# The memory's values as a group of two weight blocks with seven products

## The chip, the cores and the metric

The kernel runs on one core of a Trainium2 chip. The metric is the time of one execution on the device in microseconds, here the median of several executions. TensorE (PE in the profile) multiplies matrices, VectorE (DVE), ScalarE (ACT) and GpSimd (POOL) work elementwise, and SyncE (SP) issues most of the DMAs. Each engine takes its instructions in a fixed order from a queue of its own, and waits on semaphores for the others.

## The reference

One layer of a hybrid decoder over 256 tokens of width 2048. The part that matters here is the cross-attention into 256 memory tokens, whose keys and values come from one projection:

```python
mem_kv = rmsnorm(mem, mem_norm[l]) @ w_mem_kv[l]
m_k, m_v = jnp.split(mem_kv, 2, axis=-1)
m_k = rmsnorm(m_k.reshape(B, M, MEM_HEADS, MEM_DH), mem_k_norm[l])
m_v = m_v.reshape(B, M, MEM_HEADS, MEM_DH)
```

`w_mem_kv` is 2048 x 2048: its first 1024 columns give the keys, the last 1024 the values. After that comes the big projection of `x` (its first part is the queries for the memory, `mq`), the other mixers, the merge and the feed-forward part. All of it is float32 in and out.

## The kernel before, in words

**Numbers.** A float32 product is made of three matmuls on rounded parts: each operand is split into a high part (rounded, by an ACT copy) and a low part (the rest, by a DVE subtract), and high x high, low x high and high x low are summed in PSUM. `split` (L151, L152) does that for weights and activations.

**Plain blocks.** `gemm` multiplies 256 tokens with a block of 512 weight columns. The 2048 rows are 16 chunks of 128. A load brings four chunks (1 MB) into a slot `raw`; two chunks at a time are split into a pair of tiles `wh`, `wl` (a part, 128x1024); each part feeds 12 matmuls (two chunks, two halves of the tokens, three products) of 128x512. There are four pairs of `wh`, `wl` in this stretch, so the split of a part waits until TensorE is through with the part four places back. The `raw` slots are a list, `free_raw`: a load takes the slot that came free first. At the start these are three slots of the pool `ring1` and three borrowed places: `sh` and `sl` of the pool `fpool` (the later home of the activations' forms) and `d` of the pool `sec`.

**Groups of two blocks.** `sgemm` multiplies the same tokens with two blocks of 512 columns at once. In the first eight chunks it can replace the eight products of a 2 x 2 arrangement (two halves of the tokens or of the chunks, two halves of the chunks or blocks) by seven, over `p` chunks of each four; the remaining chunks go through `rest` as in `gemm`. For the seven products it needs sums of activations (`make_forms`: four sums and differences, each split into high and low, in a background that is woven into the code that runs beside it), sums of weights (a DVE add of 128x1024 in place, L283, or an accumulating DMA from POOL, L331 and L351), and some moves in PSUM: `put` copies or subtracts a product from a `tmp` bank into an `acc` bank or a spare piece (L314, L316). Four `acc` banks and two `tmp` banks are in use at once, and up to four `raw` slots are held until their last use.

**The order.** A scheduler that orders the instructions when the program is built works from the code's order and from its own estimates; what it made of both kernels is shown under the change.

**The stretch of the change.** First the memory's keys, two plain blocks (`o`, `o1`), while the memory's activations `mems` (tiles `oh`, `ol`) are loaded as `xraw` and split, and its row norms are made. Then the memory's values `mv`, two plain blocks (`project`), while beside them the keys are normalised and transposed, and `x` is loaded and split (`xTh`, `xTl`). Then `mq`, two plain blocks, while the forms of `x` (`sx`) are made, and from there on groups of two blocks throughout.

Of the kernel before, what the change touches and what calls it, by code (L numbers as in the profile page):

```python
# [10 lines left out]
F32R = mybir.dt.float32r  # L11
# [5 lines left out]
P = 128  # L17
# [3 lines left out]
NB = 512  # L21
# [56 lines left out]
def trunk(ctx: ExitStack, tc: tile.TileContext, a, out):  # L78
# [118 lines left out]
    def gemm(xs, w, c0, row0=0, first=(), load=nc.sync.dma_start, fine=False):  # L197

        o = [acc() for _ in range(2)]
        nk = len(xs)
        sizes = list(first)
        sizes += [min(KG, nk - k) for k in range(sum(sizes), nk, KG)]
        k0 = 0
        for n in sizes:
            xp = [x() if callable(x) else x for x in xs[k0 : k0 + n]]
            raw, done = loads()  # L210
            r0 = row0 + k0
            load(raw[:, :n], w[c0 // NB, :, r0 : r0 + n])
            for g in range(0, n, 2):
                m = min(2, n - g)
                wh, wl = (x[:].rearrange("p (k n) -> p k n", k=2) for x in parts())
                split(wh[:, :m], wl[:, :m], raw[:, g : g + m])
                if g + m == n:
                    done()
                for t in range(2):
                    s = slice(t * P, (t + 1) * P)  # L220
                    for j in range(m):
                        xh, xl = xp[g + j]
                        k = k0 + g + j
                        pe.matmul(o[t][:], xh[:, s], wh[:, j], start=k == 0, stop=False)  # L224
                        pe.matmul(o[t][:], xh[:, s], wl[:, j], start=False, stop=False)  # L225
                        pe.matmul(o[t][:], xl[:, s], wh[:, j], start=False, stop=k == nk - 1)  # L226
                    if fine and t == 0:
                        step()
                step()
            k0 += n  # L230
        return o

    def sgemm(xs, forms, w, blks, p, row0=0, late=False, moved=True, base=None, end=False):
# [56 lines left out]
            return [[x[:, t * P : (t + 1) * P] for x in xs[h * SP + i]] for i in range(SP)]  # L290

        def formed(f):
            return [[x[:, f, i] for x in forms] for i in range(SP)]

        def made():
            while id(forms) in making:
# [113 lines left out]
    def form_tiles():  # L410
        return [fpool.tile([P, 4, SP, P], F32R, name=f"s{x}", tag=f"s{x}") for x in "hl"]

    def make_forms(parts, place):

        def add(dst, a, b, op=ALU.add):
            dve.tensor_tensor(dst, a, b, op=op)

        def make():  # L420
            a = {}
            for k in range(2):
                for i in range(2):
                    at = piece()
                    a[i, k] = at[:].rearrange("p (k t) -> p k t", k=SP)
                    n = 0
                    for h, l in parts:
                        m = h.shape[1]
                        lo, hi = max(k * SP, n), min((k + 1) * SP, n + m)
                        if lo < hi:  # L430
                            add(
                                a[i, k][:, lo - k * SP : hi - k * SP],
                                *(x[:, lo - n : hi - n, i * P : (i + 1) * P].bitcast(F32) for x in (h, l)),
                            )
                        n += m
                    yield
            a11, a12, a21, a22 = a[0, 0], a[0, 1], a[1, 0], a[1, 1]
            for f, dst, x, y, op in (
                (1, a21, a22, a21, ALU.subtract),
                (3, a22, a12, a22, ALU.subtract),  # L440
                (2, a12, a21, a12, ALU.subtract),
                (0, a11, a11, a12, ALU.add),
            ):
                add(dst, x, y, op)
                yield
                split(place[0][:, f], place[1][:, f], dst)
                yield
            making.remove(id(place))

        making.add(id(place))  # L450
        background.append(make())
        return place

# [40 lines left out]
    def evac(dst, o, rstd):  # L494

        for t in range(2):
            act.activation(dst[:, t], o[t][:], AF.Copy, scale=rstd[:, t : t + 1])

    def project(dst, xs, w, c0, rstd):
        for n in range(0, MIX, NB):  # L500
            evac(dst[:, :, n : n + NB], gemm(xs, w, c0 + n), rstd)

    def normed_T(dst, src, heads, dim, gain, scratch, wait=0):


# [62 lines left out]
        return t.rearrange("p a b -> p (a b)").rearrange("p (c t) -> p c t", c=8)  # L568


    free_raw.extend([(fpool, 1, "sh"), (fpool, 1, "sl"), (sec, 1, "d")])
    mk, mkT = section("mk", "a"), chunks(section("mkT", "b")[:])
    mv, mqT = pair("mv_mqT")
    mqT = chunks(mqT)
# [10 lines left out]
    def outT():  # L585
        return [opool.tile([P, 8, T], F32R, tag="o", name=f"o{x}", bufs=4) for x in "hl"]

    mems = load_T([outT(), outT()], a["memT"], g_mem, mempool)
    cst = const.tile([P, C_R], F32, name="cst")
    cr = const.tile([P, R_W], F32R, name="cr")  # L590
    r_mem, nr_mem, r_x, nr_x = (const.tile([P, 2], F32, name=n) for n in ("r_mem", "nr_mem", "r_x", "nr_x"))
# [20 lines left out]
    dve.tensor_scalar(g_sqs[:], gain["sb_q_norm"], SD**-0.5, None, op0=ALU.mult)  # L612

    background += [token_rstd("mem", a["mem"], r_mem, nr_mem), load_consts()]
    o1 = gemm(mems, w_kv, NB)
    flush()
    evac(mk[:, :, :NB], o, r_mem)
# [7 lines left out]
    background.append(normed_T(mkT, mk, MH, MD, g_mk, lambda: mempool.tile([P, NB], F32, name="hn_sq", tag="hn")))  # L625
    background.append(load_x())
    background.append(token_rstd("x", a["x"], r_x, nr_x))
    project(mv, mems, w_kv, MIX, r_mem)
    flush()
    xs = [x() for x in xs]  # L630
    give_up(fpool)
# [98 lines left out]
    def wide(dst, c0, p=SP):  # L730
        for j, result in sgemm(xs, sx, w_in, (c0 // NB, c0 // NB + 1), p):
            for t in range(2):
                v = dst[:, t, j * NB : (j + 1) * NB]
                act.activation(v, result(t), AF.Copy, scale=r_x[:, t : t + 1])

    sx = make_forms([xtiles], form_tiles())
    mq = section("mq", "d")
    evac(mq[:, :, :NB], gemm(xs, w_in, O_MQ), r_x)
# [488 lines left out]
```

## Time and profile before

| | us |
|---|---|
| median of 3 runs | 1612.01 (1611.77 to 1614.13) |
| the profiled execution, its own time | 1609.67 |
| span of the profiled execution (first to last instruction) | 1607.9 |
| TensorE busy in the span | 1600.4 |
| VectorE busy | 1354.9 |
| ScalarE busy | 1043.8 |

The profiled execution's own time is 1.8 us over its span (launch and end), and 2.3 us under the median. A matmul's record is longer than the distance to the next one, since matmuls overlap; how fast TensorE goes is read from the starts of the rows, not from their durations. The same holds for the elementwise engines on a smaller scale: the next one starts a little before the last one's record ends.

### The profile page before, as it was taken

The page shows a single profiled execution, that of the slowest core. Times are in us where ns is not written, and L with a number is a line of the kernel's source. Part 1 is how long each engine was busy: PE and PEld are TensorE (multiplying, and loading weights), DVE is VectorE, ACT ScalarE, POOL GpSimd, SP SyncE. Part 2 cuts the span into 40 slices and gives each one's busy share as a digit, 9 for nine tenths or more (in the row PEclk, how much of TensorE's full clock was granted, in tenths as well). Part 3 has the DMA queues.
Part 4 walks back from the last instruction along what each step waited for, and adds up shares of the span by engine and source line. Part 5 has one row for each costly group of instructions (what it writes and reads, how often), then busy time and mean ns, then how long its engine had stood idle before and what let it go on. Part 6 is the DMA issues. An engine that isn't in the chain of part 4 may idle for free.

```text
span 1607.9 us, 19413 instructions
## 1 busy us (share of the span) xinstructions
PE 1600.4 (100%) x7204; PEld 1315.0 (82%) x7204; DVE 1354.9 (84%) x1544; ACT 1043.8 (65%) x1273; POOL 73.0 (5%) x95
## 2 busy tenths in 40 slices
PE   9999999999999999999999999999999999999998
PEld 7888888888888888888888888888888888888887
DVE  6777788897776788897799998988878988888996
ACT  7765677776764666665656766666666666666663
POOL 0000000000000000000000000000000000110000
PEclk9999999999999999999999999999999999999999
DMA  9765768767556878887757868777898786897684
GB/s 377 299 263 168 233 216 262 216 171 255 197 182 218 263 256 264 265 287 287 238 182 261 272 227 256 260 249 236 258 281 260 219 276 231 250 280 242 201 320 128
DMA packets 66383, 394.18 MB, mean 245 GB/s; under 512 B 7344, under 2 KB 14128, under 8 KB 21488
## 3 DMA queue, kind: packets, MB, share of 16 engines
q1 hardware_dynamic: 51344, 323.31, 52.5%
q0 software_dynamic: 11792, 66.59, 21.7%
q10 hardware_dynamic: 3152, 3.04, 0.6%
q8 instruction: 56, 0.92, 0.2%
q14 instruction: 39, 0.32, 0.1%
HBM read 324.24 MB, written 12.58 MB: 209 GB/s over the span
## 4 chain that ended last, share of the span: by engine, by line
PE 96%; DMA 2%; ACT 1%; DVE 1%; issue 0%; SPq 0%; DVEq 0%; ACTq 0%; POOLq 0%
PE acc L268 19%; PE acc L271 19%; PE acc L270 19%; PE tmp L271 7%; PE tmp L270 7%; PE tmp L268 7%; PE acc L226 5%; PE acc L225 5%; PE acc L224 5%; PE tmp L455 2%; DMA raw<-in_w_down 1%; DMA raw<-raw 0%; PE tmp L693 0%; PE tmp L721 0%; ACT wh L151 0%; DMA raw<-in_w_mem_kv 0%
## 5 line engine op out<-in xcount | busy, mean ns | idle before, releaser
L152 DVE TENSOR_TENSOR wl<-raw,wh 128x1024 fp32r<-128x1024 f32 (+1 forms) x765 | 920.1, 1221 | 209.9 <-ACT wh L151 196.6
L151 ACT CAST wh<-raw 128x1024 fp32r<-128x1024 f32 (+1 forms) x766 | 796.6, 1050 | 442.2 <-PE acc L271 225.5
L268 PE MATMUL acc<-wh,xTh 128*128 128x512 f32 x480 | 190.5, 397 | 0.0
L270 PE MATMUL acc<-wl,xTh 128*128 128x512 f32 x480 | 187.2, 390 | 0.0
L271 PE MATMUL acc<-wh,xTl 128*128 128x512 f32 x480 | 186.9, 390 | 0.0
L268 PE MATMUL acc<-wh,hh 128*128 128x512 f32 x452 | 178.8, 395 | 0.0
L270 PE MATMUL acc<-wl,hh 128*128 128x512 f32 x452 | 176.0, 389 | 0.0
L271 PE MATMUL acc<-wh,hl 128*128 128x512 f32 x452 | 175.0, 390 | 0.0
L283 DVE TENSOR_TENSOR raw<-raw 128x1024 f32<-128x1024 f32 x133 | 161.4, 1221 | 1.1 <-DMA raw<-in_w_down 0.5
L224 PE MATMUL acc<-wh,oh 128*128 128x512 f32 x320 | 126.6, 397 | 0.9 <-ACT wh L151 0.9
L225 PE MATMUL acc<-wl,oh 128*128 128x512 f32 x320 | 125.1, 391 | 0.5 <-DVE wl L152 0.5
L226 PE MATMUL acc<-wh,ol 128*128 128x512 f32 x320 | 124.8, 390 | 0.0
L268 PE MATMUL tmp<-wh,sh 128*128 128x512 f32 x294 | 115.7, 394 | 0.0
L271 PE MATMUL tmp<-wh,sl 128*128 128x512 f32 x294 | 114.7, 390 | 0.0
L270 PE MATMUL tmp<-wl,sh 128*128 128x512 f32 x294 | 114.6, 390 | 0.0
L268 PEld LDWEIGHTS acc<-wh,xTh 128*128 128x128 f32 x480 | 90.2, 188 | 20.7 <-ACT acc L314 3.1
L271 PEld LDWEIGHTS acc<-wh,xTl 128*128 128x128 f32 x480 | 90.1, 188 | 19.0
L270 PEld LDWEIGHTS acc<-wl,xTh 128*128 128x128 f32 x480 | 90.2, 188 | 17.8
L268 PEld LDWEIGHTS acc<-wh,hh 128*128 128x128 f32 x452 | 84.9, 188 | 18.6 <-ACT acc L314 1.0
L271 PEld LDWEIGHTS acc<-wh,hl 128*128 128x128 f32 x452 | 84.8, 188 | 18.0
L270 PEld LDWEIGHTS acc<-wl,hh 128*128 128x128 f32 x452 | 84.9, 188 | 16.8
L268 PE MATMUL acc<-wh,fh 128*128 128x512 f32 x220 | 86.5, 394 | 0.2 <-ACT acc L314 0.2
(311 smaller groups left out, 2322.1 us busy)
## 6 DMA issues: line engine op xcount, KB each, us to landing
raw<-in_w_gate_up SPq DMA_DIRECT2D x88, 1024.0 KB, 6.3
raw<-in_w_in SPq DMA_DIRECT2D x56, 1024.0 KB, 5.8
raw<-raw POOLq DMA_DIRECT2D x52, 1024.0 KB, 8.0
raw<-in_w_gate SPq DMA_DIRECT2D x48, 1024.0 KB, 7.4
raw<-in_w_down SPq DMA_DIRECT2D x44, 1024.0 KB, 7.2
raw<-in_w_o SPq DMA_DIRECT2D x16, 1024.0 KB, 6.2
raw<-in_w_mem_kv SPq DMA_DIRECT2D x14, 1024.0 KB, 10.5
raw<-in_w_br_mem SPq DMA_DIRECT2D x8, 1024.0 KB, 5.6
```

Source lines behind the costliest of these rows:

```text
L151: act.copy(hi, src)
L152: dve.tensor_tensor(lo, src, hi.bitcast(F32), op=ALU.subtract)
L224: pe.matmul(o[t][:], xh[:, s], wh[:, j], start=k == 0, stop=False)
L225: pe.matmul(o[t][:], xh[:, s], wl[:, j], start=False, stop=False)
L226: pe.matmul(o[t][:], xl[:, s], wh[:, j], start=False, stop=k == nk - 1)
L268: pe.matmul(dst[:], xh, wh, start=id(dst) not in begun, stop=False, skip_group_check=True)
L270: pe.matmul(dst[:], xh, wl, start=False, stop=False, skip_group_check=True)
L271: pe.matmul(dst[:], xl, wh, start=False, stop=last, skip_group_check=True)
L283: dve.tensor_tensor(x, x, y, op=ALU.add)
L455: pe.transpose(dst, src, ident)
```

## The change

The two blocks of the values become one `sgemm` group with `p` = 2: of the chunks 0 to 3 and 4 to 7, two of each four go by seven products, and the others by `rest`. `make_forms` gets the number of chunks as an argument, and the memory's forms (`smem`) are put into the background beside the second block of the keys. Their place is `sh` of `fpool`, which is no longer a `raw` slot. The sums are made in pieces of the pool `gog`; leftover pieces are dropped before the forms of `x`.

```diff
@@ sgemm, make_forms
         def formed(f):
-            return [[x[:, f, i] for x in forms] for i in range(SP)]
+            return [[x[:, f, i] for x in forms] for i in range(p)]
...
-    def make_forms(parts, place):
+    def make_forms(parts, place, p=SP):
...
-                    a[i, k] = at[:].rearrange("p (k t) -> p k t", k=SP)
+                    a[i, k] = at[:].rearrange("p (k t) -> p k t", k=SP)[:, :p]
...
-                        lo, hi = max(k * SP, n), min((k + 1) * SP, n + m)
+                        lo, hi = max(k * SP, n), min(k * SP + p, n + m)
@@ slots and tiles
-    free_raw.extend([(fpool, 1, "sh"), (fpool, 1, "sl"), (sec, 1, "d")])
+    free_raw.extend([(fpool, 1, "sl"), (sec, 1, "d")])
...
-    mems = load_T([outT(), outT()], a["memT"], g_mem, mempool)
+    mtiles = [outT(), outT()]
+    mems = load_T(mtiles, a["memT"], g_mem, mempool)
@@ before the keys' second block
+    smem = fpool.tile([P, 2, 4, 2, P], F32R, name="smem", tag="sh")
+    smem = make_forms(mtiles[:1], [smem[:, 0], smem[:, 1]], 2)
     o1 = gemm(mems, w_kv, NB)
@@ the values
-    project(mv, mems, w_kv, MIX, r_mem)
+    mems = [x() for x in mems]
+    for j, result in sgemm(mems, smem, w_kv, (MIX // NB, MIX // NB + 1), 2):
+        for t in range(2):
+            act.activation(mv[:, t, j * NB : (j + 1) * NB], result(t), AF.Copy, scale=r_mem[:, t : t + 1])
@@ before the forms of x
+    halves.clear()
     sx = make_forms([xtiles], form_tiles())
```

In the lists below, taken from the two built programs, `wh_n` and `wl_n` are the high and low part of a piece of weights, `raw_n` a load's slot, `oh`, `ol` the memory's activations and `xraw` their loads, `two` a piece that holds a sum, `smem` the forms' place.

ScalarE in the first block of the keys, from the activations of the chunks 10 and 11 on, before:

```order
L154 ACTIVATE oh_113<-xraw_235,vecs_85 128x256 x2
L151 CAST wh_243<-raw_241 128x1024
L151 CAST wh_259<-raw_241 128x1024
L154 ACTIVATE oh_113<-xraw_275,vecs_85 128x256 x2
L154 ACTIVATE oh_113<-xraw_281,vecs_85 128x256 x2
L151 CAST wh_289<-raw_287 128x1024
```

and now:

```order
L154 ACTIVATE oh_113<-xraw_235,vecs_85 128x256 x2
L151 CAST smem_325<-two_435 128x256
L151 CAST smem_325<-two_472 128x256
L151 CAST wh_243<-raw_241 128x1024
L151 CAST wh_259<-raw_241 128x1024
L154 ACTIVATE oh_113<-xraw_275,vecs_85 128x256 x2
L154 ACTIVATE oh_113<-xraw_281,vecs_85 128x256 x2
L151 CAST smem_325<-two_472 128x256
L151 CAST smem_325<-two_435 128x256
L151 CAST wh_289<-raw_287 128x1024
```

All four casts of the forms stand in the first block, two of them ahead of the cast of `raw_241`, the weights of the chunks 8 to 11.

VectorE at the same place, now (before, the rows with `two` and `smem` were not there):

```order
L152 TENSOR_TENSOR wl_214<-raw_211,wh_213 128x1024
L155 SCALAR_TENSOR_TENSOR ol_114<-xraw_229,vecs_85,oh_113 128x256 x2
L155 SCALAR_TENSOR_TENSOR ol_114<-xraw_235,vecs_85,oh_113 128x256 x2
L152 TENSOR_TENSOR smem_325<-two_435,smem_325 128x256
L418 TENSOR_TENSOR two_472<-two_472 128x256
L418 TENSOR_TENSOR two_472<-two_435,two_472 128x256
L152 TENSOR_TENSOR smem_325<-two_472,smem_325 128x256
L418 TENSOR_TENSOR two_435<-two_435,two_472 128x256
L152 TENSOR_TENSOR wl_244<-raw_241,wh_243 128x1024
```

Five rows of forms stand between the activations and the split of `raw_241`. The second cast on ScalarE above reads what the second of them (`two_472<-two_472`) writes. Before these, three more rows of forms stand between the splits of `raw_163`, `raw_187` and `raw_211` (two ahead of that of `raw_187`, one ahead of that of `raw_211`).

ScalarE at the start of the values, now; `tmp_529` is the first of the seven products, `acc_525` the bank that it is copied to:

```order
L497 ACTIVATE mk_92<-acc_326,r_mem_117 128x512
L508 ACTIVATE hn_sq_547<-mk_92 128x512
L508 ACTIVATE hn_sq_567<-mk_92 128x512
L497 ACTIVATE mk_92<-acc_327,r_mem_117 128x512
L151 CAST wh_618<-raw_573 128x1024
L314 COPY acc_525<-tmp_529 128x512
L508 ACTIVATE hn_sq_570<-mk_92 128x512
L151 CAST wh_638<-raw_531 128x1024
```

The copy is new; before, the third `hn_sq` stood directly behind the cast.

SyncE's loads at the end of the values and the start of `mq`, before (`raw_843` is the last of the values' weights, `in_x` the rows of `x` for its norm, `raw_951` the first weights of `mq`):

```order
L212 DMA raw_843<-in_w_mem_kv 128x2048
L469 DMA xraw_861<-in_xT 128x2x256
L469 DMA xraw_883<-in_xT 128x2x256
L469 DMA xraw_891<-in_xT 128x2x256
L486 DMA raw_898<-in_x 128x2048
L486 DMA raw_901<-in_x 128x2048
L469 DMA xraw_932<-in_xT 128x256
L212 DMA raw_951<-in_w_in 128x2048
L212 DMA raw_988<-in_w_in 128x2048
```

and now (`raw_881` is the last of the values' weights, `raw_991` the first weights of `mq`):

```order
L212 DMA raw_1102<-in_w_in 128x2048
L469 DMA xraw_899<-in_xT 128x2x256
L469 DMA xraw_972<-in_xT 128x256
L262 DMA raw_881<-in_w_mem_kv 128x2048
L486 DMA raw_916<-in_x 128x2048
L486 DMA raw_938<-in_x 128x2048
L212 DMA raw_991<-in_w_in 128x2048
L212 DMA raw_1028<-in_w_in 128x2048
L212 DMA raw_1065<-in_w_in 128x2048
```

A later load of `mq` (`raw_1102`, into a slot of its own) now stands ahead of the values' last weights. `raw_991` takes the slot that held block one's first four chunks (`q[11]` in the code), whose last split is that of `q4`, the seventh product in TensorE's order.

## Rows read from the trace of the kernel before

**Rows 1.** The page's first part: busy time of each engine, its share of the span, and the number of instructions.

```profile
PE 1600.4 (100%) x7204; PEld 1315.0 (82%) x7204; DVE 1354.9 (84%) x1544; ACT 1043.8 (65%) x1273; POOL 73.0 (5%) x95
```

**Rows 2.** What TensorE (PE, and its weight loads PEld) waited for: the line that waited, the one that ended the wait, us in total, times, longest. The first two are of the first 200 us, the third of the whole span.

```profile
PE acc L224 <- ACT wh L151: 0.9, 1, 0.9
PE acc L225 <- DVE wl L152: 0.5, 1, 0.5
...
PEld acc L268 <- ACT acc L314: 5.7, 17, 0.6
```

**Rows 3.** Two stretches: for PE, PEld, DVE, ACT and POOL the busy us (and instructions), then the granted TensorE clock (1.00 is 2.4 GHz), the DMA share and GB/s.

```profile
20.00:30.00 10.00, 10.00 (x46) 8.29 (x45) 6.58 (x9) 7.60 (x8) 0.00 (x0) 1.00 1.01 416
...
60.00:70.00 10.00, 10.00 (x47) 8.28 (x46) 9.86 (x19) 8.18 (x14) 0.00 (x0) 1.00 0.34 123
```

**Rows 4.** TensorE's matmuls in order of time (start, us): the first subtract-fed matmul of the part of `raw_187`, the first two rows of the part of `raw_241`, two that lie 12 matmuls apart at the start of the values, a row of four transposes, and the first of `mq`.

```profile
13.46 0.39 PE L225 MATMUL acc<-wl,oh 128*128 128x512 f32 x1
...
18.67 0.61 PE L224 MATMUL acc<-wh,oh 128*128 128x512 f32 x2
19.13 0.47 PE L225 MATMUL acc<-wl,oh 128*128 128x512 f32 x1
...
51.41 0.39 PE L224 MATMUL acc<-wh,oh 128*128 128x512 f32 x1
54.13 0.39 PE L224 MATMUL acc<-wh,oh 128*128 128x512 f32 x1
...
67.73 0.60 PE L455 MATMUL tmp<-cst,mk 128*128 128x128 f32 x4
...
96.88 0.39 PE L224 MATMUL acc<-wh,xTh 128*128 128x512 f32 x1
```

**Rows 5.** VectorE in order of time in the first block of the keys (start, us; the bracket is the idle time before it and what ended it). The splits at 9.55, 11.78, 13.88 and 17.83 are those of `raw_163`, `raw_187`, `raw_211` and `raw_241`.

```profile
9.55 1.22 DVE L152 TENSOR_TENSOR wl<-raw,wh 128x1024 fp32r<-128x1024 f32 x1 [0.92 <-ACT wh L151]
10.69 0.87 DVE L155 SCALAR_TENSOR_TENSOR ol<-xraw,vecs,oh 128x256 fp32r<-128x256 f32 x2
11.78 1.23 DVE L152 TENSOR_TENSOR wl<-raw,wh 128x1024 fp32r<-128x1024 f32 x1 [0.22 <-ACT wh L151]
12.93 0.88 DVE L155 SCALAR_TENSOR_TENSOR ol<-xraw,vecs,oh 128x256 fp32r<-128x256 f32 x2
13.88 1.23 DVE L152 TENSOR_TENSOR wl<-raw,wh 128x1024 fp32r<-128x1024 f32 x1
15.02 1.67 DVE L155 SCALAR_TENSOR_TENSOR ol<-xraw,vecs,oh 128x256 fp32r<-128x256 f32 x4
17.83 2.36 DVE L152 TENSOR_TENSOR wl<-raw,wh 128x1024 fp32r<-128x1024 f32 x2 [1.14 <-ACT wh L151]
```

**Rows 6.** ScalarE at the same time; the casts at 16.75 are those of `raw_241`.

```profile
13.75 1.70 ACT L154 ACTIVATE oh<-xraw,vecs 128x256 fp32r<-128x256 f32 x4
16.75 2.00 ACT L151 CAST wh<-raw 128x1024 fp32r<-128x1024 f32 x2 [1.29 <-DVE ol L155]
```

**Rows 7.** Groups of instructions of the first 140 us by line and shape: count, busy us, mean ns of one, idle time before them.

```profile
L152 DVE TENSOR_TENSOR wl<-raw,wh 128x1024 fp32r<-128x1024 f32 x52 | 62.9, 1223 | 29.2 <-ACT wh L151 28.7 <-issue 0.3
L151 ACT CAST wh<-raw 128x1024 fp32r<-128x1024 f32 x52 | 53.8, 1050 | 38.4 <-PE acc L226 34.7 <-DMA raw<-in_w_mem_kv 1.8 <-DVE ol L155 1.3
L155 DVE SCALAR_TENSOR_TENSOR ol<-xraw,vecs,oh 128x256 fp32r<-128x256 f32 x16 | 6.9, 480 | 0.7 <-ACT oh L154 0.7
L418 DVE TENSOR_TENSOR two<-two 128x512 f32<-128x512 f32 x4 | 2.8, 690 | 0.0
L151 ACT CAST sh<-two 128x512 fp32r<-128x512 f32 x4 | 2.4, 621 | 0.1
L169 DVE TENSOR_TENSOR rs_t<-rs_t,rs_m 128x8 f32<-128x8 f32 x4 | 0.7, 166 | 0.1
```

**Rows 8.** ScalarE where the keys' second block ends and the values begin.

```profile
50.25 0.69 ACT L497 ACTIVATE mk<-acc,r_mem 128x512 f32<-128x512 f32 x1 [0.31 <-PE acc L226]
50.97 1.16 ACT L512 ACTIVATE hn_sq<-mk 128x512 f32<-128x512 f32 x2
52.03 0.67 ACT L497 ACTIVATE mk<-acc,r_mem 128x512 f32<-128x512 f32 x1
52.60 1.04 ACT L151 CAST wh<-raw 128x1024 fp32r<-128x1024 f32 x1
53.53 0.63 ACT L512 ACTIVATE hn_sq<-mk 128x512 f32<-128x512 f32 x1
```

**Rows 9.** A group that is there already, the first after `mq`: ScalarE's copy of its first product, and TensorE around it.

```profile
144.01 0.58 ACT L314 COPY acc<-tmp 128x512 f32<-128x512 f32 x1
...
144.25 0.39 PE L270 MATMUL acc<-wl,xTh 128*128 128x512 f32 x1
144.64 0.50 PE L268 MATMUL acc<-wh,xTh 128*128 128x512 f32 x1
```

**Rows 10.** SyncE's issue of the first weights of `mq`; then landing times: loads of `raw` by source (KB each, median us from issue to landing) in the stretch 60 to 120 us and 0 to 120 us, and all loads of `raw` from 100 to 200 us.

```profile
70.97 0.33 SPq L212 DMA_DIRECT2D raw<-in_w_in  x1
...
raw<-in_w_in SPq DMA_DIRECT2D x12, 1024.0 KB, 5.2
...
raw<-in_w_mem_kv SPq DMA_DIRECT2D x14, 1024.0 KB, 10.5
...
DMA to landing us min/median/max: 4.6/6.1/9.7
```

More of the change, by code (lines that the diff above doesn't have):

```diff
@@ L497, in evac @@
             act.activation(dst[:, t], o[t][:], AF.Copy, scale=rstd[:, t : t + 1])
-    def project(dst, xs, w, c0, rstd):
-        for n in range(0, MIX, NB):
-            evac(dst[:, :, n : n + NB], gemm(xs, w, c0 + n), rstd)
     def normed_T(dst, src, heads, dim, gain, scratch, wait=0):
```

## The prediction

> **What bounds the kernel now.** Read first the busy times: TensorE is busy through all of the span, with VectorE second [rows 1]. Since matmuls overlap, that alone proves little, so read next what TensorE waited for: in the first 200 us two waits on weights, 0.9 and 0.5 us, both before 11 us (beside one for its first operand), and after that nothing [rows 2]. Then the starts: 12 matmuls take from 51.41 to 54.13, one per 0.227 us [rows 4], and the clock granted is 1.00, the 2.4 GHz level [rows 3]. The end is therefore set by the number of 128x512 matmuls at that pitch, plus each moment at which TensorE's next operand is late. A part (12 matmuls) lasts 2.72 us; its split costs ScalarE 1.05 us and VectorE 1.22 us [rows 7], so both are normally ahead. Two places are tight. In the first block the weights still come straight from the first loads [rows 5, 6]; and from 60 to 70 us VectorE is busy 9.86 of 10 us [rows 3].
>
> TensorE's weight loads are busy only 8.28 us of 10 in a stretch without any wait [rows 3]. The Trainium skill (Perfetto Trace Analysis, Identifying the Most-Contended Engine) would judge TensorE by that share rather than by matmul busy time, and so read a sixth of it as free; here that share is simply what the pitch shows when nothing is waited for, and I take TensorE as full.
>
> **The change part by part.** Everything is set against the profiled execution, 1609.67 us (span 1607.9); the median of the runs lies 2.3 us higher, at 1612.01, and the difference worked out is added to it.
>
> *Products.* Two of four chunks in eight products are 8 x 2 x 3 = 48 matmuls, seven are 42. Six fewer, at 0.227 us [rows 4]: -1.36 us. That is all the change can remove: in the values' stretch TensorE waits for nothing, so no stall can go there.
>
> *The forms' place in the first block.* Pitches first, from start to start: a 128x1024 subtract 1.14 (two take 2.36 [rows 5]), an activation's low part 0.40 (four take 1.67 [rows 5]). No 128x256 add or cast stands in the trace. VectorE's 128x512 add takes 0.69 and 128x1024 subtract 1.22 [rows 7], so a straight line gives 0.42 at 256, 0.34 to the next start; ScalarE's casts, 0.62 and 1.05 [rows 7], give 0.40 the same way. Now VectorE's queue:
> - Two adds ahead of the split of `raw_163` lie in the 0.92 us of idle before it [rows 5]: nothing.
> - Two ahead of that of `raw_187` are 0.68, less 0.22 idle [rows 5]: it begins at 12.24 instead of 11.78 and ends at 13.46, just when TensorE asks for it [rows 4]. Nothing, or a tenth.
> - One more ahead of `raw_211`: 14.55 instead of 13.88. Still ahead of TensorE by half a microsecond.
> - Then four low parts (15.7 to 17.3), a form's low part, and the add whose result ScalarE's second cast reads: done near 18.05. ScalarE, which before began the cast of `raw_241` at 16.75, when the load was there [rows 6] (the engine named in that row had long been done), now holds that cast behind the form's, until 18.5, and finishes it at 19.55. VectorE follows with the subtract until 20.8.
>
> TensorE took this subtract's result at 19.13 [rows 4] and now can at 20.85: +1.7 us. The next part is there in time, since it is needed ten matmuls later. Bounds: with forms as cheap as VectorE's smallest operations (0.17 [rows 7]) 1.1 us falls out of the chain, +0.6; with all at their 128x512 prices it grows by 1.8, +3.5. I take 1.7, the value between the two nearest sizes.
>
> *The first copy in PSUM.* In the values, count from the last matmul of the keys. In the trace the next one starts at 51.41 [rows 4]. ScalarE then runs evacuation, two squares, evacuation, cast, from 50.25 on [rows 8]; the copy comes after the cast, at 52.60 + 0.95 = 53.55. In the group after `mq` the matmul that needs such a copy started 0.63 us after the copy did [rows 9]: 54.18. With `p` = 2 TensorE has only six matmuls of the product and three others to do before that bank: 51.41 + 9 x 0.227 = 53.45. Late by 0.7 us. Such waits are on record, 5.7 us in 17 [rows 2], 0.3 on average and 0.6 the longest, with twelve matmuls in the product; bounds 0.2 and 1.1.
>
> *VectorE in the values.* It gains three subtracts and two weight sums (1.14 each), two PSUM subtracts and two adds (0.6 each): 8.1 us, in about 44 us of which it was already busy some 80 to 99% [rows 3]. The place where this shows is the copy into the second block's first bank after `p6`. From the third part's subtract to that copy VectorE has eight subtracts, two sums and two normalisations of the keys (12 x 1.14), three reductions and the copy at the 128x512 price (4 x 0.61), seven low parts (7 x 0.40) and 15 short steps (0.17): 21.5 us, starting 0.25 before the first product's start, so to 21.25. TensorE reaches the bank after 82 matmuls, 16 transposes (four: 0.60 less 0.16 overlap [rows 4]) and the 0.7 of above: 18.6 + 1.8 + 0.7 = 21.1. +0.3 us with the time of the hand-over. Bounds: 0, if the short steps hide behind long ones; 2.2, if VectorE waits on the way. The new ScalarE work (three casts, copies) is no more than 5 us and ScalarE is the less busy one: nothing.
>
> *One slot fewer, slots held.* In the first two blocks a load's slot frees 5.4 us later at most, while TensorE uses a 1 MB load in 5.4 us and five are ahead: nothing. At the end of the values it matters: before, `mq`'s first weights were issued at 70.97 for use at 96.88 [rows 4, 10]; now `raw_991` waits for the split of the seventh product. That split's cast waits for the part four places back; from there to `mq` TensorE has 48 matmuls, 10.9 us. 0.3 for the wake-up, 1.05 and 1.22 for the split, 0.1: issued 8.2 us ahead. Landing 5.2 us [rows 10], then cast and subtract, 2.4: ready about 0.6 us before its first use, and 0.2 more because the subtract is needed only by the second matmul. Nothing, but with 0.8 us left. Bounds: 0 to 3.7 (the 9.7 us landing in rows 10).
>
> *Hidden.* The two accumulating DMAs and the keys' normalisation have five parts of time or more. The forms of `x` move into `mq`, where VectorE has over half of each part free. Everything later is only re-sorted here and there, same count; worth up to 1 us either way, taken as 0.
>
> Sum: -1.36 + 1.7 + 0.7 + 0.3 + 0 = +1.3 us. 1611.0 for a profiled execution, 1613.3 for the median.
>
> **The rivals.**
> - *The cover holds.* The forms' casts find room (the load of `raw_241` lands later than 18.5, say), the copy is not late: only -1.36 is left, 1610.6. For it: TensorE hardly ever waited in the trace. Against it: ScalarE's queue is fixed, and the form's cast stands ahead.
> - *`mq`'s weights late; slower.* If `raw_991` lands more than 6.0 us after its issue, TensorE stands still at the start of `mq`. At 9.7 us that is 3.7 more than forecast: 1617.0. For it: loads of the values took 10.5 us in the median [rows 10]. Against it: those stood in a full queue (DMA share 1.01 at 20 to 30 us [rows 3]), while here only the two loads of `x` are just ahead, and in 60 to 120 us it was 5.2.
> - *TensorE has room.* If its unused sixth could take up waits, neither the six matmuls nor the 2.7 us of stalls would show: 1612.0. Against it: both stretches shown, one at the start and one later, have this same share (8.29 and 8.28 [rows 3]) as something that goes with each matmul would. The Trainium skill's rule on weight loads (Perfetto Trace Analysis, Identifying the Most-Contended Engine), weighed above, would lead here.
> - That the change does not do its work can be left out: the built program has six matmuls fewer.
>
> **How the numbers follow.** Forecast 0.60, cover holds 0.20, weights late 0.14, room in TensorE 0.06. What a measurement here can tell from no change is about 0.2%, 3.2 us. The forecast's own range, with its terms' nearer bounds, is 1611.4 to 1615.4. Low end overall: the cover case less a little, 1610.0. High end: the weights-late case, 1617.0. Faster by over 0.2% would need more than all that can be removed, 1.36 us: 0.03 for what re-sorting may do. Slower by over 0.2% (over 1615.2): most of the weights-late case and the top of the forecast, 0.15. Within: 0.82.
>
> **What would show it.** Right: a TensorE wait of 1.5 to 2 us near 19 us, ended by a cast or subtract of weights; a wait of about 0.7 us near 55 us on the PSUM copy; the first matmul on `xTh` near 98.2 instead of 96.88; no wait of TensorE there. A start of `mq` near 95.5 shows the cover case; a wait of several us ended by a cast that waited for `in_w_in` shows the late weights. The forecast is wrong if TensorE's waits up to `mq` sum to less than 1.4 us or more than 5, or if later stages differ by more than 1 us.

## The result and the profile after

The changed kernel takes 1618.97 us (median of 6, 1618.28 to 1620.42), the kernel before 1611.77 in the same comparison: ratio 1.005, 95% interval 1.0039 to 1.0061. It is slower by 7.2 us, where +1.3 was forecast, and lies above the range. The profiled execution took 1620.42 us, the longest of the six. In a second comparison (e3 below) the change costs 8.9 us, since the kernel before took 1609.66 us there and 1611.77 us here; the differences in the experiments are to be set against 8.9. Three executions in the later comparisons took 2699.8 us (kernel before), 3278.8 us (e4) and 8523.4 us (e6), and the ratios leave them out.

The page's first part, which answers to [rows 1]: six matmuls fewer, 10 instructions more on ScalarE, 21 more on VectorE.

```profile
PE 1604.3 (99%) x7198; PEld 1317.1 (81%) x7198; DVE 1366.5 (84%) x1565; ACT 1048.6 (65%) x1283; POOL 74.7 (5%) x97
```

What TensorE waited for in the whole span of the changed kernel (us in total, times, longest); [rows 2] stand against the first 200 us of it:

```profile
PE acc L224 <- ACT oh L151: 2.2, 1, 2.2
PE acc L224 <- ACT wh L151: 2.0, 1, 2.0
PE tmp L455 <- DVE mk L519: 1.3, 2, 0.8
...
PE acc L268 <- ACT acc L314: 1.0, 2, 0.6
PE tmp L855 <- DVE gaT L988: 1.0, 1, 1.0
```

Nothing of the kind of the first and the last line was in the forecast. Where they stand is seen in TensorE's rows (start, us; the bracket is the idle time and what ended it). These answer to [rows 4]:

```profile
10.67 0.73 PE L224 MATMUL acc<-wh,oh 128*128 128x512 f32 x2 [2.03 <-ACT wh L151]
...
54.14 0.39 PE L268 MATMUL tmp<-wh,oh 128*128 128x512 f32 x1
...
56.91 0.50 PE L268 MATMUL acc<-wh,oh 128*128 128x512 f32 x1 [0.57 <-ACT acc L314]
...
69.24 0.33 PE L455 MATMUL tmp<-cst,mk 128*128 128x128 f32 x1 [0.47 <-DVE mk L519]
70.37 0.55 PE L455 MATMUL tmp<-cst,mk 128*128 128x128 f32 x3 [0.81 <-DVE mk L519]
...
77.50 0.50 PE L268 MATMUL acc<-wh,oh 128*128 128x512 f32 x1 [0.18 <-DVE acc L316]
...
101.25 0.39 PE L224 MATMUL acc<-wh,xTh 128*128 128x512 f32 x1
...
433.88 1.12 PE L855 MATMUL tmp<-rb,gaT 32*128 32x512 f32 x2 [0.99 <-DVE gaT L988]
437.21 0.80 PE L224 MATMUL acc<-wh,oh 128*128 128x512 f32 x1 [2.21 <-ACT oh L151]
```

At 54.14 the values begin, at 101.25 `mq`: 4.37 us later than before (96.88 [rows 4]). From there to 429 us every row lies 4.4 us late. At 434 us two new waits come, 330 us behind the change, in a stage that the diff does not touch: the multiplication of the memory's output (`oh`) with `w_br_mem`. Stretches of 2 us there (busy us of PE, PEld, DVE, ACT, POOL with counts, then the granted clock, DMA share and GB/s):

```profile
432.00:434.00 2.00, 1.01 (x9) 0.71 (x8) 1.07 (x3) 2.00 (x5) 0.00 (x0) 1.00 0.02 8
434.00:436.00 2.00, 1.00 (x2) 0.18 (x2) 1.06 (x2) 1.97 (x4) 0.00 (x0) 1.00 0.24 86
436.00:438.00 2.00, 0.79 (x2) 0.69 (x3) 1.50 (x2) 2.00 (x3) 0.00 (x0) 0.52 0.12 45
438.00:440.00 2.00, 2.00 (x7) 1.52 (x6) 2.00 (x3) 1.05 (x2) 0.00 (x0) 0.50 0.00 0
440.00:442.00 2.00, 2.00 (x6) 1.59 (x5) 1.35 (x2) 0.63 (x1) 0.00 (x0) 0.50 0.74 172
```

ScalarE is busy 1.97 to 2.00 of each 2 us while TensorE stands still. Behind the standstill the granted clock is 0.50, the 1.2 GHz level, and 6 or 7 matmuls fall into 2 us instead of the 10 or 11 of a stretch at full clock. ScalarE's rows say what it did first:

```profile
428.31 1.05 ACT L151 CAST wh<-raw 128x1024 fp32r<-128x1024 f32 x1 [2.04 <-DMA raw<-in_w_br_mem]
429.26 0.72 ACT L772 ACTIVATE ra<-two,nr_x 128x512 f32<-128x512 f32 x1
...
435.60 0.63 ACT L775 ACTIVATE ra<-ra 128x512 f32<-128x512 f32 x1
436.13 1.98 ACT L151 CAST oh<-raw 128x1024 fp32r<-128x1024 f32 x2
```

Between 429.26 and 436.13 it works off the sigmoids of the gate; the casts of `oh`, on which TensorE waits, come behind them. In the kernel before they stand ahead of the sigmoids:

```profile
420.83 2.01 ACT L151 CAST oh<-raw 128x1024 fp32r<-128x1024 f32 x2 [0.57 <-PE acc L271]
...
423.78 0.73 ACT L769 ACTIVATE ra<-two,nr_x 128x512 f32<-128x512 f32 x1
```

Three stretches serve as a measure in what follows, each read from two rows of TensorE: the **start** (first matmul to the 96th), the **values** (first matmul of the values to the first of `mq`), the **branch** (second small product of `w_ga`, `xTl,wh`, to the first `tmp<-ra,rb`). Each is from one execution, whose own time can lie off the median: e7's is 2.1 us under its median, e11's 2.6, e1's 1.1.

| profile | start | values | branch |
|---|---|---|---|
| before | 24.00 | 45.47 | 25.73 |
| after | 26.85 | 47.11 | 31.41 |
| e1 before, count + 3 | 23.98 | 45.46 | 29.87 |
| e2 after, count - 3 | 26.74 | 47.09 | 25.42 |
| e3 after again | 26.95 | 47.20 | 29.68 |
| e5 before, one slot fewer | 25.84 | 45.48 | 25.39 |
| e6 e2, forms in `d` | 24.58 | 47.24 | 25.39 |
| e7 e2, two waits repaired | 25.09 | 47.04 | 25.41 |
| e8 e6 and e7 together | 24.69 | 47.05 | 25.43 |
| e9 e8, keys not normalised | 26.64 | 45.74 | 26.27 |
| e10 e8, `x` first | 25.92 | 45.96 | 25.43 |
| e11 before, count + 5 | 23.86 | 45.47 | 25.43 |
| e12 e6, `x` loaded by POOL | 24.62 | 45.01 | 25.40 |
| e13 e12, copy's turn too | 25.19 | 44.33 | 25.44 |

### The profile page after: what moved, and what is told of

It reads as the page before. It is cut to its first block, busy times and chain, and to the rows that moved or that the text cites. A ratio compares the mean times of both kernels' runs of the same rounds, so it can differ in the third digit from the quotient of the medians.

```text
span 1618.6 us, 19444 instructions
## 1 busy us (share of the span) xinstructions
PE 1604.3 (99%) x7198; PEld 1317.1 (81%) x7198; DVE 1366.5 (84%) x1565; ACT 1048.6 (65%) x1283; POOL 74.7 (5%) x97
## 4 chain that ended last, share of the span: by engine, by line
PE 94%; DMA 2%; DVE 2%; ACT 1%; issue 0%; SPq 0%; DVEq 0%; ACTq 0%; POOLq 0%
PE acc L268 19%; PE acc L271 19%; PE acc L270 19%; PE tmp L271 7%; PE tmp L268 7%; PE tmp L270 7%; PE acc L224 5%; PE acc L225 5%; PE acc L226 5%; PE tmp L455 2%; DVE wl L152 1%; DMA raw<-in_w_down 1%; DMA raw<-raw 1%; DMA xraw<-in_xT 0%; DMA raw<-in_w_mem_kv 0%
## 5 line engine op out<-in xcount | busy, mean ns | idle before, releaser
L224 PE MATMUL acc<-wh,oh 128*128 128x512 f32 x256 | 102.9, 405 | 4.2 <-ACT oh L151 2.2
L225 PE MATMUL acc<-wl,oh 128*128 128x512 f32 x256 | 101.9, 398 | 0.5 <-DVE wl L152 0.5
L226 PE MATMUL acc<-wh,ol 128*128 128x512 f32 x256 | 101.4, 397 | 0.0
```

## The experiments

**The count (e1, e2, e11).** The parts' tiles come from a list of pairs, `splits`, and a counter, `turn` (L182), deals them out. From the second block of `mq` on the list has six entries, four of `ring1` and two of `ring_a`. The values took 16 parts before and take 19 now (seven of the products, twelve of `rest`). So later on each part lies in another pair; in the built programs the memory that `oh` takes over from `ring_a` comes free 18 matmuls (4.1 us) before the end of the gate's group in the kernel before, and with the group's last matmul now, together with the sigmoids' input. The order then puts the sigmoids first. e1 moves only the count in the kernel before, e2 moves it back in the changed kernel:

```diff
@@ e1: kernel before
+    turn[0] += 3
     sx = make_forms([xtiles], form_tiles())
@@ e2: changed kernel
     halves.clear()
+    turn[0] -= 3
     sx = make_forms([xtiles], form_tiles())
```

> The kernel before, with nothing of the change but one thing that the change does on the side: the count that deals the weight parts over the pairs of tiles is moved on by three after the values (the change makes 19 parts there instead of 16). From mq on every engine's order is then that of the changed kernel; up to there it is that of the kernel before. Theory A (the count decides which piece of memory comes free last before the branch stage, and so puts the branch's operand behind the sigmoids on ScalarE): 5 to 6.5 us slower than before, about 1617.5, with a TensorE wait of 3 to 4 us near 428 us and a granted clock of 0.5 for some 6 us behind it. Rival B (all is lost in the first 100 us, by the forms and the group): no change, within 1 us of before.

> The changed kernel with the count moved back by three after the values; from mq on the order is that of the kernel before. Theory A: 1612.5 to 1614, 5 to 6.5 us faster than the changed kernel, no wait near 430 us; about 1 to 2 us over the kernel before, the local stretch of the values alone. Rival B: as the changed kernel, about 1619.

Measured: e1 1615.13 us against 1609.66 for the kernel before on the same chip, ratio 1.0033 (1.0021 to 1.0046), that is +5.5. e2 1613.12, ratio 1.002 (1.0012 to 1.0029); the changed kernel as it is took 1618.53 there (e3), so the count gives back 5.4. TensorE's waits in e1, and the stretch behind them:

```profile
429.42 1.12 PE L853 MATMUL tmp<-rb,gaT 32*128 32x512 f32 x2 [0.50 <-DVE gaT L986]
432.72 0.57 PE L224 MATMUL acc<-wh,oh 128*128 128x512 f32 x1 [2.18 <-ACT oh L151]
```

```profile
432.00:434.00 2.00, 1.28 (x4) 0.98 (x5) 1.76 (x3) 2.00 (x3) 0.00 (x0) 0.75 0.00 1
434.00:436.00 2.00, 2.00 (x6) 1.59 (x5) 2.00 (x3) 0.81 (x2) 0.00 (x0) 0.50 0.00 0
436.00:438.00 2.00, 2.00 (x9) 1.59 (x8) 0.85 (x1) 1.02 (x2) 0.00 (x0) 0.90 0.95 262
```

The same two waits, the same clock, without forms or group. In e2 the same two rows of TensorE have no wait before them:

```profile
434.25 1.12 PE L856 MATMUL tmp<-rb,gaT 32*128 32x512 f32 x2
435.30 0.50 PE L224 MATMUL acc<-wh,oh 128*128 128x512 f32 x1
```

Theory A holds on both sides: by the medians 5.4 of the loss are the count's. Not all of its figures came true: the waits in e1 sum to 2.7 us, not 3 to 4, and e2 stays 3.5 us over the kernel before, not 1 to 2. In the profiled executions the branch itself is longer than before by 4.1 us (e1), 4.0 (e3) and 5.7 (after); where the rest of the 5.4 lies in the other executions is not shown.

e11 tries another turn of it, `turn[0] += 5`.

> The kernel before with the count moved on by five instead of three (e1): by its order only the second of the two casts of the branch's operand stands behind the sigmoids on ScalarE, the first ahead of them, and six matmuls stay between the last small product and that of the gate. Theory A (the place of these two casts is what costs): TensorE has 24 matmuls of the first four chunks, 5.4 us, before it needs the second half, so the wait near 430 us is under 1 us and the time within 1 us of the kernel before. If any turn of the count other than the one before costs, as e1: 4 us or more.

Measured: 1614.73 against 1609.75, ratio 1.0029 (1.0019 to 1.0039). The branch costs nothing (25.43), as theory A had it, yet the kernel is 5.0 slower. In the profiled execution (2.5 us slower than that of the kernel before) there is a new loss at the start of the feed-forward part, where TensorE was 0.6 us ahead of the kernel before up to 910 us and is 2.7 behind it at 922 (TensorE's rows there):

```profile
918.02 0.73 PE L268 MATMUL acc<-wh,hh 128*128 128x512 f32 x2 [2.11 <-ACT wh L151]
919.37 0.50 PE L270 MATMUL acc<-wl,hh 128*128 128x512 f32 x1 [0.61 <-DVE wl L152]
```

The kernel before has no such wait there. So the expected time was wrong, and the lesson is wider than e1's: the two other turns of the count that were tried each have a late place of their own.

**The start (e3, e4, e5, e6).** e3 and e4 repeat the changed kernel and the kernel before.

> The changed kernel as it is, for a second profile of it. If the later landing of the third load of the memory's activations (8.29 us instead of 7.20) and the halved clock from 12.8 to 16.4 us belong to the change, they come again and mq begins near 101.2 us; if they belong to that one execution, the first cast after the wait begins near 8.5 us, the clock stays at 1.00 there, and mq begins 2 to 3 us earlier, at 98.5 to 99.5. The wait near 434 us and the clock of 0.5 behind it come again in either case.

> The kernel before as it is, for a second profile of its start. If the loads of the start vary from run to run, the first matmul fed by the third pair of activations (9.57 us in the first profile) moves by up to 1 us; if they don't, it stays within 0.2 us.

e3: 1618.53, ratio 1.0052 (1.0038 to 1.0066). The late first matmul of the third part came again (10.67), the 1.2 GHz behind it did not, and `mq` begins at 101.33 all the same; so the lost time at the start is not the clock's alone. The load that was late was not the same one: the activations are read at 7.60, and the cast of the weights waits for its own load until 9.57. Of e4 (3278.81 us) only the first microseconds can be used: the third load of activations is read at 6.34 there, at 7.20 in the first profile, so these loads vary from run to run. In e3, with TensorE at full clock, the wait of the forecast comes at 20.55, in the part where it was put, and again in e7, whose third load of activations came early (used at 6.20, the third part at 8.85; TensorE's rows of e7):

```profile
17.93 0.39 PE L226 MATMUL acc<-wh,ol 128*128 128x512 f32 x1
18.94 0.73 PE L224 MATMUL acc<-wh,oh 128*128 128x512 f32 x2 [0.62 <-ACT wh L151]
20.20 0.50 PE L225 MATMUL acc<-wl,oh 128*128 128x512 f32 x1 [0.53 <-DVE wl L152]
20.53 0.39 PE L226 MATMUL acc<-wh,ol 128*128 128x512 f32 x1
```

From start to start the three rows from 18.94 on come 0.78, 0.81 and 0.10 later than the pitch: 1.7 us. In the changed kernel's own profile this wait is absent; TensorE was slower ahead of it there, at a clock of 0.70 and 0.50 from 12 to 16 us.

e5 takes only the slot away in the kernel before; e6 puts the forms in `d` and gives `sh` back to the first block.

```diff
@@ e5: kernel before
-    free_raw.extend([(fpool, 1, "sh"), (fpool, 1, "sl"), (sec, 1, "d")])
+    free_raw.extend([(fpool, 1, "sl"), (sec, 1, "d")])
@@ e6: e2
-    free_raw.extend([(fpool, 1, "sl"), (sec, 1, "d")])
+    free_raw.extend([(fpool, 1, "sh"), (fpool, 1, "sl"), (sec, 1, "d")])
...
-    smem = fpool.tile([P, 2, 4, 2, P], F32R, name="smem", tag="sh")
+    free_raw.remove((sec, 1, "d"))
+    smem = sec.tile([P, 2, 4, 2, P], F32R, name="smem", tag="d")
```

> The kernel before with one edit of the change alone: the place sh is no longer a slot for loads, so the fourth load goes into sl and the fifth into d. Every engine's order stays as it is. In three profiles with the order of before the third load of activations was used at 6.3 to 7.2 us, in three of changed kernels at 7.6 to 8.3. Theory S (the places into which the first loads go make this difference): activations at 7.5 to 8.3 us, the first matmul of the third part at 10.4 to 10.7 instead of 9.6, often a halved clock behind it; 1.5 to 2.8 us slower than before. Rival F (something of the forms or of the longer program makes it): as before within 0.5 us, and 9.6 us again.

> The kernel of e2 (count moved back), with the forms in the place d, after its last load, instead of sh, so that there are six slots again for the first block; the forms' casts then come behind both casts of raw_241 on ScalarE. The adds of the forms stay in the first block. Theory S: the start is that of before (9.6 us, clock 1.00) and no wait near 20 us; 2 to 2.7 us faster than e2, 1610.4 to 1611.1. If the slots are not it, 10.5 us again and the time of e2 within 0.7; if only the held cast matters (a wait of 0.6 us near 20 us in the second profile of the changed kernel), 0.6 faster.

e5: 1609.76, ratio 0.9997 (0.9988 to 1.0006): theory S falls, and with 10.01 us for the third part in its profile also the thought that only changed kernels start late. Over all profiles this row lies at 9.36 to 10.01 us with the order of before and at 8.85 to 10.67 with changed ones; whether the change moves its mean stays open. e6: 1611.76, ratio 1.0007 (0.9998 to 1.0017), 1.4 under e2 by the differences to the kernel before: more than a held cast of 0.6, less than theory S. Of the 1.7 us near 19 us it still has 0.75 (0.64 and 0.11 over the pitch); the casts are behind `raw_241` now, the adds are not. The same edit lies between e7 and e8 below, in one comparison, and is worth 2.7 us there, as much as theory S had said. So the forms' place costs the changed kernel 1.4 to 2.7 us, while e5 shows that the slot alone costs the kernel before nothing; the rows account for 0.95 of it, and the rest stays open.

**Single waits of the values (e7, e8, e9).** e7 puts the transposes three steps later and turns the two halves of the first `rest` part round; e8 adds e6 to it; e9 leaves the normalisation out.

```diff
@@ e7: e2
-def normed_T(dst, src, heads, dim, gain, scratch, wait=0):
+def normed_T(dst, src, heads, dim, gain, scratch, wait=0, gap=1):
...
-        yield
+        for _ in range(gap):
+            yield
...
-            for t in range(2):
+            for t in (1, 0) if swap and (j, k) == (0, SP + p) else (0, 1):
@@ e9: e8, for the keys alone (norm is False; squares and sums left out likewise)
...
-        y = rsqrt_mean(ss[:].rearrange("p t h -> p (t h)"), dim, 2 * heads)
+        y = rsqrt_mean(ss[:].rearrange("p t h -> p (t h)"), dim, 2 * heads) if norm else None
         for t in range(2):
+            if not norm:
+                yield
+                continue
```

> The kernel of e2 with two repairs in the values: three steps more between the normalisation of the keys and their transposes, and the first rest part begins with the other half of the tokens, so that TensorE comes to the copied bank six matmuls later. The waits of 0.7 us on the copy and of 1.5 us on the normalised keys go: 2.0 to 2.2 us faster than e2, 1610.9 to 1611.1. If the time these waits take were given back elsewhere (VectorE being full there), less than 1 us.

> All repairs together: count moved back, forms in d, transposes later, first rest part turned. By the sum of the terms 1613.1 - 2.1 - 2.5 = 1608.5, that is the kernel before less the six matmuls (1.36 us) and the put's 0.3: ratio to before 0.999. If VectorE's load in the values is a limit of its own, it ends above the kernel before.

> The kernel of e8 with the normalisation of the keys left out (their squares, sums, reciprocal root and scaling: four reductions, 15 short steps and two 128x1024 products on VectorE, four squares on ScalarE); the transposes and all matmuls stay, so the output is not the reference's. From the first matmul of the values to the first of mq the kernel before takes 45.47 us, the changed kernel and e2, e6, e7, e8 47.0 to 47.2, whatever wait was repaired. If VectorE's work in that stretch is the limit, these 3 us of waits go: 44.1 to 44.4 us for the stretch (45.47 less the six matmuls), some 2.5 to 3 us faster than e8. If a wait of its own kind (put, weights) holds TensorE, 46 us or more.

e7: 1614.32, ratio 1.0025 (1.0014 to 1.0036), 4.6 over the kernel before and no better than e2. e8: 1611.58, ratio 1.0014 (1.0005 to 1.0023), that of e6. Both expectations missed: the waits on the copy and on the keys are gone, and the time is back at the next place, where TensorE needs the copy of the sixth product, p6, into the second block's first bank (e8, then e9):

```profile
73.85 0.50 PE L268 MATMUL acc<-wh,oh 128*128 128x512 f32 x1 [1.77 <-DVE acc L316]
```

```profile
74.15 0.50 PE L268 MATMUL acc<-wh,oh 128*128 128x512 f32 x1 [1.36 <-DVE acc L316]
```

e9: 1610.35, ratio 1.0006 (0.9996 to 1.0015), values 45.74, between the two figures of its expectation (44.4 and 46): without any normalisation 1.6 us of the 3.0 over 44.11 (45.47 less the six matmuls) remain. So VectorE's work is not all of it; something also comes to it late. The rows of the changed kernel show what: SyncE's issues, then ScalarE, then VectorE.

```profile
41.84 16.14 SPq L262 DMA_DIRECT2D raw<-in_w_mem_kv  x3
58.03 4.10 SPq L469 DMA_DIRECT2D xraw<-in_xT  x4
```

```profile
65.73 1.14 ACT L154 ACTIVATE xTh<-xraw,vecs 128x256 fp32r<-128x256 f32 x2 [2.67 <-DMA xraw<-in_xT]
```

```profile
64.23 0.16 DVE L168 SCALAR_TENSOR_TENSOR rs_t<-rs_y 128x8 f32<-128x8 f32 x1
66.27 0.48 DVE L155 SCALAR_TENSOR_TENSOR xTl<-xraw,vecs,xTh 128x256 fp32r<-128x256 f32 x1 [1.88 <-ACT xTh L154]
66.67 0.16 DVE L169 TENSOR_TENSOR rs_t<-rs_t,rs_m 128x8 f32<-128x8 f32 x1
...
67.96 2.36 DVE L519 TENSOR_TENSOR mk<-mk,rs_y 128x1024 f32<-128x1024 f32 x2
```

The first load of `x` is issued at 58.03, behind weight loads that take from 41.84 to 58 to get their slots; in the kernel before it was issued at 41.50. Its landing holds ScalarE for 2.67 us, VectorE's `xTl` holds it up for 1.88 in the middle of the normalisation of the keys, and everything queued behind, needing no `x` at all, is late: the keys, p6's copy. The Trainium skill (Perfetto Trace Analysis, Tensor Engine Instruction) calls these engines strict FIFO; the trace agrees: `rs_t`, whose operands were there at 64.4, starts at 66.67. How far the delay reaches is seen in e8, where VectorE has no idle time between these two rows:

```profile
64.16 0.49 DVE L155 SCALAR_TENSOR_TENSOR xTl<-xraw,vecs,xTh 128x256 fp32r<-128x256 f32 x1 [1.94 <-ACT xTh L154]
...
73.11 0.69 DVE L316 TENSOR_TENSOR acc<-two,tmp 128x512 f32<-128x512 f32 x1
```

Without the idle time the copy at 73.11 could have come up to 1.94 us earlier; TensorE waits 1.77 us for it.

**The order of `x`'s loads (e10, e12, e13).** e10 puts the loads of `x` first in the background and the normalisation last, and takes e7's three steps out; e12 is e6 with the loads of `x` issued by POOL; e13 is e12 with the turned halves of e7.

```diff
@@ e10: the values' background
-    background.append(normed_T(mkT, mk, MH, MD, g_mk, ...))
     background.append(load_x())
     background.append(token_rstd("x", a["x"], r_x, nr_x))
+    background.append(normed_T(mkT, mk, MH, MD, g_mk, ...))
@@ e12: load_T
-                (nc.scalar if g == 0 and src is a["memT"] else nc.sync).dma_start(
+                (nc.gpsimd if src is a["xT"] else nc.scalar if g == 0 and src is a["memT"] else nc.sync).dma_start(
```

> The kernel of e8 with another order in the values' background, and with the one step of before ahead of the transposes: the loads and splits of x first, the normalisation of the keys last; VectorE then does the 15 short steps and the two products behind the copy of p6 instead of ahead of it, and as much of x's splits ahead. Same work, moved by some 15 us. If it is the pile of work ahead of p6's copy that costs, the stretch falls to 44.5 to 45.5 us and the kernel is 1.5 to 2.5 us faster than e8, at or just under the kernel before (1608.5 to 1610). If x's splits fill the same place, 46.5 to 47.2 and no gain.

> The kernel of e6 with one edit: the loads of x are issued by POOL instead of SyncE. Theory D: in the values x's first load is issued at 58.0 us instead of 41.5, because six weight loads that wait for slots stand ahead of it in SyncE's queue; ScalarE's xTh then waits 2.7 us for its landing, VectorE's first xTl 1.9 us behind it, and the last steps of the keys' normalisation behind that, so that the transposes (1.6 us of waits) and p6's copy come late. By POOL the load is issued before 50 us, the waits on the normalised keys and on p6's copy go, the wait on the first copy (0.7) stays: values to mq 44.8 to 45.2 us instead of 47.2, and 2 us faster than e6, 1609.4 to 1610.2. Rival (VectorE is simply full, whatever comes first, as e7 to e9 let one think): 46.5 us or more and less than 0.8 us gained.

> e12 with the first rest part turned as in e7. By theory D the wait on the first copy goes too: values to mq 44.1 to 44.5 us (45.47 less the six matmuls is 44.11), 0.7 us faster than e12; less than half a microsecond from the kernel before, on its faster side if the forms' place in the first block (0.75 us left near 19.5 us) costs no more: 1608.8 to 1609.6.

e10: 1610.27, ratio 1.0001 (0.9992 to 1.001), 1.3 under e8 (1.5 to 2.5 were expected) and level with the kernel before; values 45.96, a half more than expected. e12 and e13 take 45.01 and 44.33 us for the values, as theory D had it (44.8 to 45.2; 44.1 to 44.5), with no wait on keys or p6's copy; in e12 0.57 us of idle time on the first copy is left, in e13 none. But they took away more than the late load. With `x` there early, all 16 of its splits run before the values begin, and VectorE has less to do there. The stretch of the values in e6, e12, e9 and e13 (length, then busy us of PE, PEld, DVE, ACT, POOL with counts, clock, DMA share, GB/s):

```profile
51.76:99.00 47.24, 45.01 (x204) 36.32 (x202) 38.02 (x70) 35.74 (x52) 1.86 (x2) 1.00 0.77 263
...
58.08:103.09 45.01, 44.44 (x203) 36.34 (x202) 32.11 (x54) 29.76 (x36) 1.77 (x2) 1.00 0.67 228
...
53.92:99.66 45.74, 44.38 (x204) 36.36 (x202) 32.55 (x47) 34.32 (x49) 1.85 (x2) 1.00 0.81 265
...
56.99:101.32 44.33, 44.33 (x203) 36.33 (x202) 32.39 (x56) 30.11 (x37) 1.77 (x2) 1.00 0.68 232
```

So e12 alone does not part theory D from its rival, a full VectorE. Two comparisons do better. e9 and e13 leave VectorE as little to do (32.55 and 32.39 us); the load of `x` is late in e9 alone, and its values are 1.4 us longer. In e10 the load is issued at 41.16, VectorE is busier than in e8 (40.16 us against 38.27), and the values are 1.1 us shorter. By the first pair the late load is worth 1.4 us of the 2.7 between e8 and e13; e10, which moved the normalisation too, only agrees with that. The other 1.3 went with VectorE's work (e8 to e9), and what each costs while the other is there is not shown.

The whole kernels are nevertheless slower, 1615.43 (1.0035, 1.0021 to 1.0049) and 1614.1 (1.0028, 1.0016 to 1.0039), against the expectation: POOL, which waits only for the slots of `xraw`, issues `x` from 11.48 to 30.44 us, among the loads of the keys' weights (rows of POOL and TensorE in e12):

```profile
11.48 0.71 POOL L469 DMA_DIRECT2D xraw<-in_xT  x1 [11.04 <-DVE ol L155]
...
30.44 0.58 POOL L469 DMA_DIRECT2D xraw<-in_xT  x1 [2.46 <-DVE xTl L155]
```

```profile
39.23 0.73 PE L224 MATMUL acc<-wh,oh 128*128 128x512 f32 x2 [3.49 <-ACT wh L151]
```

The cast that ends this wait starts at 38.13 on ScalarE, behind a wait of 2.23 us for the memory's rows (`in_mem`, used at 34.62) and three activations of `x`; the clock then falls to 0.64 and 0.51 from 40 to 44 us. From the 96th matmul to the values TensorE takes 28.17 us (26.69 in e13) instead of e6's 21.99: the gain of 2.2 us in the values is paid for almost three times over. No version tried beats the kernel before. e10 equals it, and by the differences to the kernel before it lies 8.3 us under the changed kernel's e3; e6 (1.0007) cannot be told from it either.

## Why the prediction was wrong

- **"Everything later is only re-sorted here and there, same count; worth up to 1 us either way, taken as 0."** This step failed, and it is most of the error: 5.4 to 5.5 us by e1 and e2. The count of matmuls was the same; the count of parts dealt before them was not, and with it the memory that `oh` waits for. The moved casts stood in the order of the two programs. The prediction's own sign of being wrong, later stages that differ by more than 1 us, came: the branch took 31.41 us instead of 25.73.
- **"One slot fewer, slots held ... nothing" and "Hidden".** This failed too. Only the loads of weights were followed there, not those of `x` queued behind them on SyncE. The first came 16.5 us later, and with it waits on the keys, 1.7 us by the starts (1.3 of idle time), that were no term of the sum at all. The values took 47.11 us where 45.47 - 1.36 + 1.0 = 45.1 was forecast: 2.0 missing. VectorE's busy time in the values is what it was (38.20 us against 38.04 before, since the sums for the forms of `x` moved on into `mq`), so the amount alone is no reason for a wait; what changed is where the work stands. How much of the 2.0 is the late load and how much the work queued in that place is shown only in part (e9, e10, e13).
- **Products, -1.36.** Right: e13's stretch is 1.14 us under that of before, with no wait in its rows; the 0.2 short of the term is not traced.
- **Forms in the first block, +1.7 near 19 us.** Right in place and size where TensorE came at full clock (e3, e7); the straight line's 0.42 and 0.40 for an add and a cast of 128x256 were measured as 0.42 and 0.39 to 0.41. About 0.95 of it can be had back (e6). Beside it the third part began 0.9 to 1.1 us late from a load in three profiles (after, e2, e3), in two of them with 1.2 GHz behind it, which runs did not tie to the change.
- **First copy, +0.7.** Right: 0.57 of idle time, 0.72 by the starts, and gone with the turned halves (e7).
- **p6's copy, +0.3.** 0.35 by the starts, right in size by luck: VectorE idled 1.88 us ahead of it, waiting for `xTh`, which the forecast had only as a bound, and TensorE came late itself by the waits on the keys.
- **`mq`'s weights, nothing.** Right: the first load was issued at 92.91, 8.3 us before `mq` (8.2 forecast), and TensorE didn't wait.
- **The rivals.** Cover holds and late weights did not come. Room in TensorE fell: e1's waits of 0.5 and 2.2 us cost 4.1 us, more than their length.

Without the count the forecast would have been +3.5 (e2) against +1.3 said: the right sign, less than half the size, and the values are 2.0 of the missing 2.2 us.

## What to carry to other kernels

Where tiles are dealt out by a running counter, a change in the number of parts shifts the home of every later part; at each place where one pool's memory goes over to another, ask which instruction now frees it last, before calling the rest "the same". Read what is queued behind a load that waits for a slot, on the issuing engine and then on each engine in order that needs the data: a late load that nobody awaits yet can hold work that never touches it. Repairing single waits tells little when they have one cause upstream. A repair that moves the cause tells more, but look at what else it moves: e12 brought the load forward and took a sixth of VectorE's work out of the stretch with it.

## What the runs showed of the hardware

A wait can cost more than its length when the clock falls behind it: in the changed kernel the two waits at 434 us hold 3.2 us of idle time, and the branch takes 5.7 us more than before, with the clock at 0.52, 0.50 and 0.50 behind them; in e3 waits of 2.7 us cost 4.0. At the start nearly the same wait was followed by 1.2 GHz in one execution (2.03 us, changed kernel, 12 to 16 us) and not in another (1.82 us, e3). And in e4, an execution of the kernel before, the matmuls lie 0.47 us apart instead of 0.227 with the granted clock shown as 1.00, so that column alone does not vouch for the engine's speed.
